# Moving the right-hand tiles of a hybrid encoder layer by 384 bytes, and small edits at its first transfers, at a pass border and at its last gates

## The chip, the cores and the metric

The kernel runs on one core of one Trainium2 chip. The metric is device time in microseconds (us) of one execution. Five engines work side by side and meet only at semaphores: PE (matrix products into PSUM), DVE (vector), ACT (scalar functions and copies), POOL and SP. SP, ACT and POOL also issue DMA transfers, each to its own queue. A product has a stationary operand, loaded into the array ahead of it (the view calls that PEld), and a moving operand that is streamed past it.

## The reference, cut to what matters

```python
h    = rms_norm(x, norm_w)                              # x: 512 tokens x 2048, float32
proj = einsum('bsd,de->bse', h, w_in)                   # w_in: 2048 x 4608
q, k, v, g_attn, xr, g_lru = split(proj)
attn = softmax(rope(norm(q)) rope(norm(k))^T / sqrt(128)) v      # 8 heads, 2 kv heads, 128 wide
lru  = scan_forward(conv(xr)) + scan_backward(conv(xr))          # gated linear recurrences
mixed = concat([rms_norm(attn, attn_norm_w) * silu(g_attn),
                rms_norm(lru,  lru_norm_w)  * silu(g_lru)])      # 512 x 2048
out  = x + einsum('bse,ed->bsd', mixed, w_out)          # w_out: 2048 x 2048
```

Everything is float32. silu(g) is g times sigmoid(g).

## The kernel before, in words

**Three products for one.** An operand in float32 is split into a rounded high part (a copy into `float32r`, mostly on ACT) and the rest (a subtraction on DVE). Each product of 128x128 by 128x512 is then three matmuls: high by high, high by low, low by high. Names with `h` are high parts, with `l` low parts: `wh`/`wl` of weights, `oh`/`ol` of operands of the output product, `mh`/`ml` of the mixed activations, `x2` (shown as `x`) of the input.

**Stages.** The kernel turns x and projects the recurrence input (`proj_feat`), then runs the other projections (`proj_feat`, `proj_tok`) with the recurrence, the rotary embedding and the attention woven into them as work of ACT and DVE, and last the output product (`outputs`). The weights of a chunk come in 512 KB transfers into three `wr` tiles. PE's order is written out by hand for the whole program (`manual_schedule`); SP's at the start, and ACT's, DVE's and SP's in the output stage; elsewhere a scheduler with priorities orders ACT and DVE.

**The first transfers.** `xload` and `wraw` load the first 256 columns of x and the first 256 rows of weights in two halves each: x on SP's queue, weights on ACT's, and the norm weights `nw_st` on ACT's between the two weight halves. PE first runs 13 matmuls on `ones` (`busy(WARM)`) that compute nothing needed, turns `nw_st` into columns (`columns`), turns the first x block (`xturn`), runs 6 more on `ones`, and then begins `proj_feat` (L292).

**The output stage.** It is a seven-product scheme on 2x2 blocks. `seven` and `combine` make seven combinations of each of eight pairs of activations (`build`, the left operands `mh`, `ml`: pairs 0 to 3 lie in pool `fin`, 4 in a ring of pool `hq`, 5 to 7 in pool `out`). Two column groups g of the output are made in two passes each: `P1, Q6, Q5, Q7` and then `P2, Q3, Q4`. `uses` gives the order of the uses: pair i, product k; a use is six matmuls (two strips of 128 tokens, three matmuls each), except that pairs 6 and 7 are kept to the end of each product. `operand` makes the moving operand of use n in the tile n mod 7: tiles 0 to 2 are in `fin`, 3 to 6 in `out`. `prepare` runs six uses ahead. When a product is finished, `done` adds its bank into the output tiles `xt` on DVE. The gates of the last four heads and the left operands 5, 6 and 7 are made by DVE and ACT inside the first pass (`last_gates`), one step at each new pair of the first product.

**Addresses.** Pools are allocated from the left (`cp`, `wr`, `xw`, later `out`) and from the right end (`end`, `hq`, `lru`, `qkv`, `att`, `wx`, `fin`) of each partition's memory. In the built program the tiles of `wr`, `xw` and `out` start at multiples of 512 bytes. Below `end` (24 floats) nearly all tiles of the right-hand pools have remainder 384 after division by 512 (`k2` of pool `att`: 192). So two operands of one matmul can differ in this remainder: a weight from `wx` (right) with `x2` of `xw` (left), or `mh` of `fin` with `oh` of `out`.

Of the kernel before, what the change touches and what calls it, by code (L numbers as in the profile page):

```python
# [11 lines left out]
F32 = mybir.dt.float32  # L12
# [25 lines left out]
AHEAD = 600  # L38


WARM, WARM2 = 13, 6


STEPS = 2
# [12 lines left out]
def hybrid_kernel(  # L57
# [27 lines left out]
    def opened(name, side):  # L85
        pools[name] = tc.alloc_tile_pool(name=name, bufs=1, side=side, reuse_waits="tile")
        order[side].append(name)
        return pools[name]
# [8 lines left out]
    cp = opened("cp", "left")  # L97
    opened("wr", "left")
    opened("xw", "left")
    opened("end", "right").tile([P, 24], F32, tag="end", name="end")  # L100
    hring = opened("hq", "right").ring(8 * 2048, name="hring")
    aring = pools["hq"].ring(8 * 2048, name="aring")
    opened("lru", "right")
# [81 lines left out]
        return vec[:, r : r + 1]  # L185


    def wraw(w, r0, c0, nk=1, queue=nc.sync):

        raw = pools["wr"].tile([P, 2, SEQ], F32, tag="wr", bufs=3, name=nm("wr"))  # L190
        src = w[r0 : r0 + 2 * P, c0 : c0 + SEQ].rearrange("(k p) e -> p k e", p=P)
        for k in range(nk):
            ks = slice(k * 2 // nk, (k + 1) * 2 // nk)
            queue.dma_start(raw[:, ks, :], src[:, ks, :])
            yield raw

    turn_of = [0]

    def wsplit(raw, k):

        turn_of[0] += k
        pool = pools["wx" if "wx" in pools and turn_of[0] % 2 else "xw"]
        hi = pool.tile([P, SEQ], F32R, tag="wh", bufs=4, name=nm("wh"))
        lo = pool.tile([P, SEQ], F32R, tag="wl", bufs=4, name=nm("wl"))
        nc.scalar.copy(hi, raw[:, k, :])  # L205
        nc.vector.tensor_sub(lo, raw[:, k, :], f(hi))  # L206
        return hi, lo

# [6 lines left out]
    xh, xl = [None] * KT, [None] * KT  # L215
    ssq = const([P, NT, KT // 2], "ssq")

    def xload(c, nk=1):

        xc = b4(shape=(P, NT, 2 * P))  # L220
        for k in range(nk):
            ks = slice(k * 2 * P // nk, (k + 1) * 2 * P // nk)
            cs = slice(c * 2 * P + ks.start, c * 2 * P + ks.stop)
            nc.sync.dma_start(xc[:, :, ks], xf[:, cs].rearrange("(t p) d -> p t d", p=P))
            yield xc

    def xturn(xc, kk):
# [339 lines left out]
    def weights(q, g, t):  # L567

        qh, ql = q
        tt = slice(t * P, (t + 1) * P)  # L570
        sc = mm()
        mm3(sc, qh[:, tt], ql[:, tt], kth[g], ktl[g], True, True)
        mx = pools["att"].tile([P, 1], F32, tag="mx", bufs=6, name=nm("mx"))
        nc.vector.tensor_reduce(mx, sc, axis=AX.X, op=ALU.max, negate=True)  # L574
        p = k2()
        sm = pools["att"].tile([P, 1], F32, tag="sm", bufs=6, name=nm("sm"))
        nc.scalar.activation(p, sc, AF.Exp, bias=mx, accum_out=sm)
        nc.vector.reciprocal(sm, sm)
        nc.gpsimd.tensor_scalar(p, p, sm, 0.0, op0=ALU.mult, op1=ALU.add)
        return p  # L580
# [112 lines left out]
    def seven(src, op, hi, lo):  # L693

        src = halves(src)
        res = combine(src, op)
        for to, part in ((slice(0, 3), src[:, 1:4]), (slice(3, 7), res)):
            nc.scalar.copy(hi[:, to], part)
            nc.vector.tensor_sub(lo[:, to], part, f(hi[:, to]))

    def kept(pool, n=7):
        return [pool.tile([P, n, H], F32R, tag=t, bufs=1, name=t) for t in (nm("mh"), nm("ml"))]
# [91 lines left out]

    kept_c = {}
    PASS = (((0, "P1"), (5, "Q6"), (4, "Q5"), (3, "Q7")), ((2, "P2"), (6, "Q3"), (1, "Q4")))
    TAIL = 2

    def uses():

# [39 lines left out]

    def outputs(work):

        bank, tmp, at = {}, {}, [0]

        def take(key):
            bank[key] = pj() if at[0] % 8 >= 4 else mm()
            at[0] += 1
            return bank[key]

        def tm(tag, s):  # L850
            tmp[tag, s] = fin_ev()
            return tmp[tag, s]

        def fin_ev():
            return pools["fin"].tile([P, SEQ], F32, tag="ev", bufs=4, name=nm("ev"))

        def done(g, name, s):

            xt = xts[g]
            b00, b01 = xt[s][:, :SEQ], xt[s][:, SEQ:]  # L860
            b10, b11 = xt[2 + s][:, :SEQ], xt[2 + s][:, SEQ:]
            v = nc.vector
            if name == "P1":
                nc.scalar.copy(tm("a", s), bank[name, s])
                v.tensor_add(b11, b11, tmp["a", s])
            elif name == "Q6":
                v.tensor_sub(tm("b", s), bank[name, s], tmp["a", s])
                v.tensor_sub(b01, b01, tmp["b", s])
            elif name == "Q5":
                v.tensor_add(tm("c", s), bank[name, s], tmp["b", s])  # L870
                v.tensor_add(b00, b00, tmp["c", s])
            elif name == "Q7":
                v.tensor_add(b00, bank[name, s], b00)
                store(g, s, 0)
                v.tensor_sub(b01, b01, bank[name, s])
                v.tensor_add(b10, b10, tmp["c", s])
            elif name == "P2":
                v.tensor_add(b11, bank[name, s], b11)
                store(g, 2 + s, 1)
            elif name == "Q3":  # L880
                v.tensor_add(b10, bank[name, s], b10)
                store(g, 2 + s, 0, queue=nc.sync if g else None)
            elif g == 0 or s == 0:
                v.tensor_add(b01, bank[name, s], b01)
                store(g, s, 1, queue=nc.sync if g else None)
            else:
                for h in range(2):
                    hs = slice(h * H, (h + 1) * H)
                    v.tensor_add(b01[:, hs], bank[name, s][:, hs], b01[:, hs])
                    store(g, s, 1, hs, nc.sync)  # L890

        def mult(use, s):

            g, second, k, i = use
            a, name = PASS[second][k]
            ah, al = mixed[i][1]
            bh, bl = ready[use]
            ts_ = slice(s * P, (s + 1) * P)
            if i == 0:
                take((name, s))  # L900
            for j, (lh, rh) in enumerate(((ah, bh), (ah, bl), (al, bh))):
                nc.tensor.matmul(  # L902
                    bank[name, s], lh[:, a, ts_], rh, start=i == 0 and j == 0,
                    stop=i == 7 and j == 2,
                )
            if i == 7:
                done(g, name, s)

        for n, use in enumerate(order_):
            g, second, k, i = use  # L910
            prepare(n + NW - 1)
            if (second, k, i) == (0, 0, 3):
                xts.setdefault(g, None)
                xts[g] = xts[g] or residual_tiles()
                residual(g)
            if g == 0 and not second and k == 0:
                next(work, None)
            if i < 8 - TAIL:
                for s in range(2):
                    mult(use, s)  # L920
            elif i == 7:
                for s in range(2):
                    for m in range(8 - TAIL, 8):
                        mult((g, second, k, m), s)
# [19 lines left out]
    )  # L944
    given = {}
    with tc.high_priority():
        xs, ws = xload(0, 2), wraw(w_in, 0, C_XR, 2, nc.scalar)
        xc, raw = next(xs), next(ws)
        nc.scalar.dma_start(nw_st, norm_w.rearrange("(k p) -> k p", p=P))
        next(xs), next(ws)  # L950
        table = const([P, 1], "table")
        nc.scalar.activation(table, ones[:, :1], AF.Exp)
        columns(nw, nw_st)
        first = [wsplit(raw, 0)]
        xturn(xc, 0)
        busy(WARM2)
    chunks = [xchunk(c) for c in range(1, KT // 2)]
# [99 lines left out]

    def build(i, pair, where):
        mixed[i][1] = hi, lo = where(7)
        seven(pair, ALU.subtract, hi, lo)  # L1060

    for q in range(4):
        for _ in range(2):
            next(fill, None)
        build(q, hp[q], lambda n: kept(pools["fin"]))
    drain(fill)


    def later():
        for pair in ap_[:2]:  # L1070
            normed(pair)
        yield 6
        todo = gate(late, ap_[:2], R_AN, fin_s)
        for _ in range(3):
            yield next(todo)
        build(4, ap_[0], lambda n: [hring.tile([P, n, H], F32R, name=nm(t)) for t in ("mh", "ml")])
        yield from todo
        for pair in ap_[2:]:
            normed(pair)
# [13 lines left out]
        prepare(NW - 1)  # L1093

    def last_gates():
        yield
        build(5, ap_[1], lambda n: last_mixed[0])
        yield
        todo = gate(gs, ap_[2:], R_AN + 4, fin_s)
        for _ in range(3):  # L1100
            next(todo)
        yield
        build(6, ap_[2], lambda n: last_mixed[1])
        drain(todo)
        yield
        build(7, ap_[3], lambda n: last_mixed[2])
        yield

    with tc.manual_schedule(
        engines={mybir.EngineType.Activation, mybir.EngineType.DVE, mybir.EngineType.SP}  # L1110
# [45 lines left out]
```

## Time and profile before

| | us |
|---|---|
| three runs | 658.4, 656.95, 658.29 |
| median | 658.29 |
| the profiled execution | 657.07 |
| its span from the first to the last instruction | 655.3 |

The profile is of one execution. Times inside it count from the start of its span. "Busy" of PE holds the modelled ends of matmuls; the distance between the starts of two matmuls says more, and the chain of waits shows it: a piece of it lasts from its own start to the next one's.

### The profile page before, as it was taken

Reading aid. Unit: us, or ns where it says so; the run is one execution under the profiler, and the core shown is the slowest. Engines: PE = TensorE matmul, PEld = TensorE weight load, DVE = VectorE, ACT = ScalarE, POOL = GpSimd, SP = SyncE. Lnnn points to the kernel's source line nnn. Section 1 sums busy time; section 2 is a strip of 40 time slices with the busy share of each in tenths; the row PEclk is TensorE's granted clock in tenths of the full one; section 3 lists DMA queues with packets and bytes.
Section 4 is the critical chain, followed back from the end, with each engine's and each line's share of the span. In section 5 each row is a group of like instructions: output and inputs, shape, how many; then the busy total and the mean of one; then the engine's idle time right before and its main releaser. Section 6 shows DMA issues by size and latency. Waiting matters only on the chain.

```text
span 655.3 us, 8600 instructions
## 1 busy us (share of the span) xinstructions
PE 647.8 (99%) x2960; PEld 532.1 (81%) x2960; DVE 485.8 (74%) x832; ACT 344.4 (53%) x639; POOL 96.5 (15%) x127
## 2 busy tenths in 40 slices
PE   8999999999999999999999999999999999999997
PEld 6888888888888888888888888888888878888875
DVE  5778679977687925855955568439948997698994
ACT  3543799489856515454735456335434564344441
POOL 0000000000022312132543435411000000100000
PEclk9999999999999999999999999999999999999999
DMA  9933253322334331446776678663355667585322
GB/s 292 312 107 113 65 139 95 98 65 65 97 114 129 95 98 33 122 141 147 170 177 149 196 150 193 151 144 111 96 191 197 256 208 248 179 297 177 131 78 96
DMA packets 53067, 96.96 MB, mean 148 GB/s; under 512 B 4316, under 2 KB 14688, under 8 KB 52896
## 3 DMA queue, kind: packets, MB, share of 16 engines
q1 hardware_dynamic: 45648, 75.17, 36.2%
q0 software_dynamic: 7056, 20.72, 13.6%
q10 hardware_dynamic: 320, 0.53, 0.3%
q8 instruction: 23, 0.38, 0.2%
q14 instruction: 20, 0.16, 0.1%
HBM read 92.21 MB, written 20.98 MB: 173 GB/s over the span
## 4 chain that ended last, share of the span: by engine, by line
PE 96%; DVE 1%; DMA 1%; issue 1%; ACT 0%; ACTq 0%; DVEq 0%
PE pj L146 20%; PE pj L148 20%; PE pj L147 20%; PE mm L902 12%; PE pj L902 9%; PE mm L146 3%; PE mm L148 3%; PE mm L147 3%; PE mm L586 2%; PE mm L231 1%; PE pj L292 1%; PE mm L534 1%; DMA nw_st<-in_norm_w_dram 1%; DVE ol L717 0%; DMA rw<-in_w_out_dram 0%
## 5 line engine op out<-in xcount | busy, mean ns | idle before, releaser
L146 PE MATMUL pj<-x,wh 128*128 128x512 f32 x376 | 150.5, 400 | 0.0
L148 PE MATMUL pj<-x,wl 128*128 128x512 f32 x376 | 146.8, 390 | 0.0
L147 PE MATMUL pj<-x,wh 128*128 128x512 f32 x376 | 146.6, 390 | 0.0
L205 ACT CAST wh<-wr 128x512 fp32r<-128x512 f32 x144 | 86.1, 618 | 70.4 <-PE pj L148 26.2
L206 DVE TENSOR_TENSOR wl<-wr,wh 128x512 fp32r<-128x512 f32 x144 | 98.7, 706 | 29.7 <-ACT wh L205 29.7
L148 PEld LDWEIGHTS pj<-x,wl 128*128 128x128 f32 x376 | 70.6, 188 | 15.3
L147 PEld LDWEIGHTS pj<-x,wh 128*128 128x128 f32 x376 | 70.8, 188 | 13.5
L146 PEld LDWEIGHTS pj<-x,wh 128*128 128x128 f32 x376 | 70.7, 188 | 13.5
L146 PE MATMUL pj<-wh,x 128*128 128x512 f32 x192 | 75.3, 392 | 0.0
L148 PE MATMUL pj<-wh,x 128*128 128x512 f32 x192 | 75.2, 392 | 0.0
L147 PE MATMUL pj<-wl,x 128*128 128x512 f32 x192 | 75.1, 391 | 0.0
L716 ACT CAST oh<-rw 128x512 fp32r<-128x512 f32 x94 | 54.8, 619 | 32.6 <-PE mm L902 17.7
L717 DVE TENSOR_TENSOR ol<-rw,oh 128x512 fp32r<-128x512 f32 x94 | 60.6, 686 | 9.7 <-ACT oh L716 6.7
L902 PE MATMUL mm<-ol,mh 128*128 128x512 f32 x128 | 50.3, 393 | 0.5 <-DVE ol L717 0.5
L902 PE MATMUL mm<-oh,mh 128*128 128x512 f32 x128 | 50.2, 392 | 0.0
L902 PE MATMUL mm<-oh,ml 128*128 128x512 f32 x128 | 50.2, 392 | 0.0
L588 ACT CAST pt<-mm 128x512 fp32r<-128x512 f32 x32 | 18.7, 586 | 52.7 <-PE mm L586 52.7
L147 PEld LDWEIGHTS pj<-wl,x 128*128 128x128 f32 x192 | 36.1, 188 | 7.9
L146 PEld LDWEIGHTS pj<-wh,x 128*128 128x128 f32 x192 | 36.0, 188 | 7.9
L148 PEld LDWEIGHTS pj<-wh,x 128*128 128x128 f32 x192 | 36.0, 188 | 7.9
L574 DVE TENSOR_REDUCE mx<-mm 128x1 f32<-128x512 f32 x32 | 22.1, 690 | 23.9 <-PE mm L148 23.4
L902 PE MATMUL pj<-ol,mh 128*128 128x512 f32 x96 | 37.9, 394 | 0.0
(207 smaller groups left out, 1110.2 us busy)
## 6 DMA issues: line engine op xcount, KB each, us to landing
wr<-in_w_in_dram SPq DMA_DIRECT2D x71, 512.0 KB, 3.7
rw<-in_w_out_dram SPq DMA_DIRECT2D x63, 256.0 KB, 3.7
ts<-in_w_out_dram POOLq DMA_DIRECT2D x24, 512.0 KB, 6.5
rw<-ts SPq DMA_DIRECT2D x31, 256.0 KB, 4.9
ts<-ts POOLq DMA_DIRECT2D x8, 512.0 KB, 6.1
xt<-in_x_dram SPq DMA_DIRECT2D x8, 512.0 KB, 8.9
b<-in_x_dram SPq DMA_DIRECT2D x7, 512.0 KB, 8.0
out_dram<-xt POOLq DMA_DIRECT2D x12, 256.0 KB, 3.4
```

The costliest lines, as they stand in the source:

```text
L146: nc.tensor.matmul(acc, lh, rh, start=start, stop=False)
L147: nc.tensor.matmul(acc, lh, rl, start=False, stop=False)
L148: nc.tensor.matmul(acc, ll, rh, start=False, stop=stop)
L205: nc.scalar.copy(hi, raw[:, k, :])
L206: nc.vector.tensor_sub(lo, raw[:, k, :], f(hi))
L231: nc.tensor.transpose(pt[:, t * P : (t + 1) * P], xc[:, t, ks], ident)
L574: nc.vector.tensor_reduce(mx, sc, axis=AX.X, op=ALU.max, negate=True)
L586: nc.tensor.transpose(pt[:, s * P : (s + 1) * P], p[:, s * P : (s + 1) * P], ident)
L588: nc.scalar.copy(pth[:, :, tt], p3)
L716: nc.scalar.copy(hi, src)
L717: nc.vector.tensor_sub(lo, src, f(hi))
L902: nc.tensor.matmul(bank[name, s], lh[:, a, ts_], rh, start=i == 0 and j == 0, stop=i == 7 and j == 2,)
```

## The change

It makes these edits:

- `end` grows from 24 to 120 floats, and `mx` and `sm` get 16 buffers instead of 6. In the built program every 512-wide matmul's operands then start at a multiple of 512 bytes.
- The first transfers: the first half of x and then the first half of the weights on SP's queue; `nw_st`, the second half of x and the second half of the weights on ACT's.
- Matmuls on `ones`: 9, 1 and 4 instead of 13 and 6; the 1 stands between `columns` and the first turn of x.
- The first `wh` is copied by DVE instead of ACT.
- In `done` for Q7 the addition of `c` into `b10` is held back and made at the second and third use of the next pass.
- `seven` stops after its combination and after each of its two parts; `last_gates` runs in 13 pieces over the first 22 uses.
- The last four gates: silu on ACT and one DVE operation, instead of sigmoid and two.

```diff
-WARM, WARM2 = 13, 6
+WARM, WARM1, WARM2 = 9, 1, 4
...
-    opened("end", "right").tile([P, 24], F32, tag="end", name="end")
+    opened("end", "right").tile([P, 120], F32, tag="end", name="end")
...
-        for k in range(nk):
+        nk = len(queues)
+        for k, queue in enumerate(queues):
             ks = slice(k * 2 // nk, (k + 1) * 2 // nk)
             queue.dma_start(raw[:, ks, :], src[:, ks, :])
...
-        mx = pools["att"].tile([P, 1], F32, tag="mx", bufs=6, name=nm("mx"))
+        mx = pools["att"].tile([P, 1], F32, tag="mx", bufs=16, name=nm("mx"))
...
         res = combine(src, op)
+        yield
         for to, part in ((slice(0, 3), src[:, 1:4]), (slice(3, 7), res)):
             nc.scalar.copy(hi[:, to], part)
             nc.vector.tensor_sub(lo[:, to], part, f(hi[:, to]))
+            yield
...
-    TAIL = 2
+    TAIL, PIECES, LAST_USE = 2, 13, 22
...
-                v.tensor_add(b10, b10, tmp["c", s])
+                held.append((b10, tmp["c", s]))
...
-            if g == 0 and not second and k == 0:
+            if second and k and held:
+                b10, c = held.pop(0)
+                nc.vector.tensor_add(b10, b10, c)
+            if n * PIECES // LAST_USE != (n - 1) * PIECES // LAST_USE:
                 next(work, None)
...
-        xs, ws = xload(0, 2), wraw(w_in, 0, C_XR, 2, nc.scalar)
+        queues = nc.sync, nc.scalar
+        xs, ws = xload(0, queues), wraw(w_in, 0, C_XR, queues)
+        nc.scalar.dma_start(nw_st, norm_w.rearrange("(k p) -> k p", p=P))
         xc, raw = next(xs), next(ws)
-        nc.scalar.dma_start(nw_st, norm_w.rearrange("(k p) -> k p", p=P))
         next(xs), next(ws)
...
-        first = [wsplit(raw, 0)]
+        busy(WARM1)
+        first = [wsplit(raw, 0, nc.vector.tensor_copy)]
...
     def last_gates():
...
+        yield from build(5, ap_[1], lambda n: last_mixed[0])
+        for i in (6, 7):
+            for e in range(2):
+                k = 2 * (i - 6) + e
+                sg, dst = fin_s(), ap_[i - 4][:, e, :]
+                nc.scalar.activation(sg, gs[k], AF.Silu)
+                nc.vector.scalar_tensor_tensor(
+                    dst, dst, v1(R_AN + 4 + k), sg, op0=ALU.mult, op1=ALU.mult
+                )
+                yield
+            yield from build(i, ap_[i - 4], lambda n: last_mixed[i - 5])
```

The order of ACT at the start, before the change (`wr` are weights as loaded, `nw_st` the norm weights, `table` a dummy that loads ACT's function table):

```order
L194 DMA wr_142<-in_w_in_dram 128x512
L949 DMA nw_st<-in_norm_w_dram 16x128
L194 DMA wr_142<-in_w_in_dram 128x512
L952 ACT_TABLE_LOAD
L952 ACTIVATE table<-ones 128x1
L205 CAST wh_152<-wr_142 128x512
L233 ACTIVATE x_24_161<-mm_156,nw 128x512
```

The same place after the change:

```order
L956 DMA nw_st<-in_norm_w_dram 16x128
L226 DMA b_18_137<-in_x_dram 128x4x128
L195 DMA wr_139<-in_w_in_dram 128x512
L960 ACT_TABLE_LOAD
L960 ACTIVATE table<-ones 128x1
L235 ACTIVATE x_24_158<-mm_153,nw 128x512
L206 CAST wh_174<-wr_139 128x512
```

The norm weights have moved ahead of everything on ACT's queue, the first weights have left it for SP's queue, half of x has come to it, and the first cast of weights has left ACT for DVE.

The order of DVE at the border between the two passes of the second column group, before the change (`xt` are the output tiles, `pj` the finished product Q7, `ol` a low part that PE waits for, `tc` a sum of weight blocks):

```order
L717 TENSOR_TENSOR ol_5828<-rw_5820,oh_5827 128x512
L873 TENSOR_TENSOR xt_5581<-pj_5465,xt_5581 128x512
L875 TENSOR_TENSOR xt_5581<-xt_5581,pj_5465 128x512
L876 TENSOR_TENSOR xt_5583<-xt_5583,ev_5806 128x512
L873 TENSOR_TENSOR xt_5582<-pj_5469,xt_5582 128x512
L875 TENSOR_TENSOR xt_5582<-xt_5582,pj_5469 128x512
L876 TENSOR_TENSOR xt_5584<-xt_5584,ev_5815 128x512
L717 TENSOR_TENSOR ol_5852<-tc_5416,oh_5851 128x512
L717 TENSOR_TENSOR ol_5868<-rw_5863,oh_5867 128x512
L791 TENSOR_TENSOR tc_5474<-tc_5474,rw_5863 128x512
L717 TENSOR_TENSOR ol_5881<-rw_5865,oh_5880 128x512
```

The same place after the change:

```order
L721 TENSOR_TENSOR ol_5819<-rw_5811,oh_5818 128x512
L877 TENSOR_TENSOR xt_5572<-pj_5456,xt_5572 128x512
L879 TENSOR_TENSOR xt_5572<-xt_5572,pj_5456 128x512
L877 TENSOR_TENSOR xt_5573<-pj_5460,xt_5573 128x512
L879 TENSOR_TENSOR xt_5573<-xt_5573,pj_5460 128x512
L721 TENSOR_TENSOR ol_5841<-tc_5407,oh_5840 128x512
L721 TENSOR_TENSOR ol_5857<-rw_5852,oh_5856 128x512
L922 TENSOR_TENSOR xt_5574<-xt_5574,ev_5797 128x512
L795 TENSOR_TENSOR tc_5465<-tc_5465,rw_5852 128x512
L721 TENSOR_TENSOR ol_5871<-rw_5854,oh_5870 128x512
L922 TENSOR_TENSOR xt_5575<-xt_5575,ev_5806 128x512
```

The two additions of `ev` (L876) stood ahead of the first `ol` of the new pass; they now stand behind the second and the third.

PE's order differs only in the matmuls on `ones`, and POOL's not at all.

More of the change, by code (lines that the diff above doesn't have):

```diff
@@ L185, in v1, with wraw @@
         return vec[:, r : r + 1]
-    def wraw(w, r0, c0, nk=1, queue=nc.sync):
+    def wraw(w, r0, c0, queues=(nc.sync,)):
         raw = pools["wr"].tile([P, 2, SEQ], F32, tag="wr", bufs=3, name=nm("wr"))
         src = w[r0 : r0 + 2 * P, c0 : c0 + SEQ].rearrange("(k p) e -> p k e", p=P)
-        for k in range(nk):
+        nk = len(queues)
+        for k, queue in enumerate(queues):
             ks = slice(k * 2 // nk, (k + 1) * 2 // nk)
@@ L197, in hybrid_kernel, with wsplit @@
     turn_of = [0]
-    def wsplit(raw, k):
+    def wsplit(raw, k, rounded=nc.scalar.copy):
         turn_of[0] += k
@@ L204, in wsplit @@
         lo = pool.tile([P, SEQ], F32R, tag="wl", bufs=4, name=nm("wl"))
-        nc.scalar.copy(hi, raw[:, k, :])
+        rounded(hi, raw[:, k, :])
         nc.vector.tensor_sub(lo, raw[:, k, :], f(hi))
@@ L216, in hybrid_kernel, with xload @@
     ssq = const([P, NT, KT // 2], "ssq")
-    def xload(c, nk=1):
+    def xload(c, queues=(nc.sync,)):
         xc = b4(shape=(P, NT, 2 * P))
-        for k in range(nk):
+        nk = len(queues)
+        for k, queue in enumerate(queues):
             ks = slice(k * 2 * P // nk, (k + 1) * 2 * P // nk)
             cs = slice(c * 2 * P + ks.start, c * 2 * P + ks.stop)
-            nc.sync.dma_start(xc[:, :, ks], xf[:, cs].rearrange("(t p) d -> p t d", p=P))
+            queue.dma_start(xc[:, :, ks], xf[:, cs].rearrange("(t p) d -> p t d", p=P))
             yield xc
@@ L572, in weights @@
         mm3(sc, qh[:, tt], ql[:, tt], kth[g], ktl[g], True, True)
-        mx = pools["att"].tile([P, 1], F32, tag="mx", bufs=6, name=nm("mx"))
+        mx = pools["att"].tile([P, 1], F32, tag="mx", bufs=16, name=nm("mx"))
         nc.vector.tensor_reduce(mx, sc, axis=AX.X, op=ALU.max, negate=True)
         p = k2()
-        sm = pools["att"].tile([P, 1], F32, tag="sm", bufs=6, name=nm("sm"))
+        sm = pools["att"].tile([P, 1], F32, tag="sm", bufs=16, name=nm("sm"))
         nc.scalar.activation(p, sc, AF.Exp, bias=mx, accum_out=sm)
@@ L841, in outputs @@
     def outputs(work):
-        bank, tmp, at = {}, {}, [0]
+        bank, tmp, at, held = {}, {}, [0], []
         def take(key):
@@ L1059, in build @@
         mixed[i][1] = hi, lo = where(7)
-        seven(pair, ALU.subtract, hi, lo)
+        return seven(pair, ALU.subtract, hi, lo)
     for q in range(4):
@@ L1064, in hybrid_kernel @@
             next(fill, None)
-        build(q, hp[q], lambda n: kept(pools["fin"]))
+        drain(build(q, hp[q], lambda n: kept(pools["fin"])))
     drain(fill)
@@ L1075, in later @@
             yield next(todo)
-        build(4, ap_[0], lambda n: [hring.tile([P, n, H], F32R, name=nm(t)) for t in ("mh", "ml")])
+        drain(
+            build(4, ap_[0], lambda n: [hring.tile([P, n, H], F32R, name=nm(t)) for t in ("mh", "ml")])
+        )
         yield from todo
@@ L1095, in last_gates @@
     def last_gates():
[L1096 to L1107, printed above, removed]
+        yield from build(5, ap_[1], lambda n: last_mixed[0])
[6 more added lines that the diff above has]
+                    dst, dst, v1(R_AN + 4 + k), sg, op0=ALU.mult, op1=ALU.mult
+                )
+                yield
+            yield from build(i, ap_[i - 4], lambda n: last_mixed[i - 5])
     with tc.manual_schedule(
```

## The prediction

> **What bounds the kernel now.** I read the page's busy time and its chain first: where must a gain come from?
>
> ```profile
> PE 647.8 (99%) x2960; PEld 532.1 (81%) x2960; DVE 485.8 (74%) x832; ACT 344.4 (53%) x639; POOL 96.5 (15%) x127
> PE 96%; DVE 1%; DMA 1%; issue 1%; ACT 0%; ACTq 0%; DVEq 0%
> ```
>
> The first row is busy time of each engine, the second the shares of the chain that ended last. Almost all of the span is PE doing matmuls one behind the other. An edit can only shorten the pace of the matmuls, the few gaps between them, the start, or the end. Next, the chain in the output stage, in order of time: start, length, engine and bank, count. Two uses are 12 matmuls.
>
> ```profile
> 495.19 2.72 PE mm L902 x12
> 497.92 2.75 PE pj L902 x12
> 500.67 2.80 PE mm L902 x12
> 503.47 2.77 PE pj L902 x12
> 506.24 2.72 PE mm L902 x12
> 508.96 2.79 PE pj L902 x12
> 511.75 2.80 PE mm L902 x12
> 514.55 2.73 PE pj L902 x12
> ...
> 645.64 5.47 PE mm L902 x24
> 651.11 0.02 issue
> ```
>
> PE waits for nothing here, yet the same 12 matmuls take 2.72 or 2.80 us, and the pattern is that of the addresses. In these uses the stationary `mh` is always a right-hand tile (remainder 384). The moving `oh` and `ol` of use n are right-hand where n mod 7 is 0, 1 or 2, else left-hand (remainder 0). Row by row, uses with equal remainders: 2 of 2 (n = 0, 1), 1 of 2, 0 of 2, 1 of 2, 2 of 2, 0, 0, 2 of 2. The times follow: 2.72, 2.75, 2.80, 2.77, 2.72, 2.79, 2.80, 2.73. Banks don't (both sorts stand at `mm` and at `pj`). So a matmul costs 2.72/12 = 226.7 ns where both operands start at the same remainder, and 2.80/12 = 233.3 ns where not: 6.6 ns apart.
>
> **The change part by part.** *Addresses.* Afterwards both operands of every 512-wide matmul start at a multiple of 512, so I take 226.7 ns for all. What that is worth, stage by stage, with these rows (windows: length, PE busy and count, the other engines; groups: count, busy, mean ns):
>
> ```profile
> 190.00:260.00 70.00, 70.00 (x317) 57.01 (x316) 45.28 (x85) 36.20 (x107) 16.47 (x24) 1.00 0.32 94
> L148 PE MATMUL pj<-wh,x 128*128 128x512 f32 x95 | 37.5, 394 | 0.0
> L902 PE MATMUL mm<-oh,mh 128*128 128x512 f32 x128 | 50.2, 392 | 0.0
> L902 PE MATMUL pj<-ol,mh 128*128 128x512 f32 x96 | 37.9, 394 | 0.0
> L146 PE MATMUL mm<-kt,b 128*128 128x512 f32 x32 | 12.6, 395 | 0.0
> ```
>
> Output stage: 3 x 128 + 3 x 96 = 672 matmuls from 495.19 to 651.11, 155.9 us. At 226.7 ns they take 152.3. Of the 3.6 us between, 0.8 are the stall below, so 2.8 are pace. From 190 to 260 us weights lie in turn in the right-hand `wx` and the left-hand `xw`; some 283 matmuls (three lines of about 95), so between half and all of them at 6.6 ns: 0.9 to 1.9 us. I take 1.2, nearer to half, since half the weights are in `wx`. Attention: 96 score matmuls with `kt` right-hand and the left operand `b` at remainder 0, 96 x 6.6 ns = 0.6; I take 0.5. Other stages have few such pairs. Sum **4.5 us**; the bounds are 0 (the remainder only goes along with something else) and 5.3. A loss is excluded by the 2.72 rows, in which the remainders are equal already.
>
> A rule of the Trainium skill speaks against this term. SBUF — State Buffer, "Operand start alignment", asks only for a start at a multiple of the element's size, and "Who interferes with whom" gives PE two independent read ports, one for the moving operand and one for the weights, and says that PE never waits on anyone. By it this term would be 0; the trace's 2.72 against 2.80 us does not agree.
>
> *Two additions behind the pass border.* The only stall of PE in the middle of the program is here:
>
> ```profile
> 620.45 0.68 DVE L873 TENSOR_TENSOR xt<-pj,xt 128x512 f32<-128x512 f32 x1
> 621.05 0.68 DVE L875 TENSOR_TENSOR xt<-xt,pj 128x512 f32<-128x512 f32 x1
> 621.64 0.69 DVE L876 TENSOR_TENSOR xt<-xt,ev 128x512 f32<-128x512 f32 x1
> 622.25 0.68 DVE L873 TENSOR_TENSOR xt<-pj,xt 128x512 f32<-128x512 f32 x1
> 622.85 0.68 DVE L875 TENSOR_TENSOR xt<-xt,pj 128x512 f32<-128x512 f32 x1
> 623.44 0.69 DVE L876 TENSOR_TENSOR xt<-xt,ev 128x512 f32<-128x512 f32 x1
> 624.04 0.69 DVE L717 TENSOR_TENSOR ol<-tc,oh 128x512 fp32r<-128x512 f32 x1
> 623.86 0.39 PE L902 MATMUL mm<-oh,mh 128*128 128x512 f32 x1
> 624.78 0.50 PE L902 MATMUL mm<-ol,mh 128*128 128x512 f32 x1 [0.54 <-DVE ol L717]
> ```
>
> Two matmuls start 0.92 us apart instead of 0.23: a loss of 0.69, and the one behind restarts slowly, some 0.1 more. Without the two L876 rows, which each hold DVE for 0.60 until the next start, `ol` ends at about 624.73 - 1.20 = 623.53, ahead of the 624.09 at which PE wants it. Behind it the additions come back: next `ol` to 624.1, addition to 624.7, `tc` to 625.3, third `ol` to 625.9. PE wants that third one for the use that begins at 623.86 + 2 x 1.39 = 626.6. Nothing is late next. Gain **0.7 us**, bounds 0.3 (a new small wait) and 0.8.
>
> *The start.* Timeline rows (start, length) and DMA issues (KB, us from issue to landing):
>
> ```profile
> 1.13 2.96 PE L935 MATMUL mm<-ones 128*128 128x256 bf16 x13 [1.13 <-POOL ones L154]
> 1.18 0.45 ACTq L949 DMA_DIRECT2D nw_st<-in_norm_w_dram  x1
> 5.55 0.20 PE L180 MATMUL mm<-ident,nw_st 16*128 16x16 f32 x1 [1.46 <-DMA nw_st<-in_norm_w_dram]
> 6.17 0.82 PE L935 MATMUL mm<-ones 128*128 128x256 bf16 x6
> 6.38 0.69 ACT L233 ACTIVATE x<-mm,nw 128x512 fp32r<-128x512 f32 x1 [1.30 <-PE mm L231]
> 7.12 1.20 PE L292 MATMUL pj<-x,wh 128*128 128x512 f32 x4
> wr<-in_w_in_dram ACTq DMA_DIRECT2D x1, 256.0 KB, 3.7
> b<-in_x_dram SPq DMA_DIRECT2D x2, 256.0 KB, 4.8
> ```
>
> The norm weights, issued at 1.18 behind 256 KB, hold PE until 5.55; x had landed by then. Issued first on ACT's queue they land long before x. The first half of x stays first on SP's queue. It lands between 4.4 (3.7 us after issue, like the first weights) and 5.5; I take 4.7. Then 0.6 of turning and 0.7 of ACT put `x` at 6.0. The weights now stand second on SP's queue, where x's second half stood, which landed 4.8 us after 1.23, at 6.1. DVE's copy adds at most 0.69 (like the subtraction rows above): `wh` between 5.7 and 6.8. The first needed matmul then starts between 6.0 and 6.8 instead of 7.12; I take 6.5, a gain of **0.6 us**, bounds -0.3 (the weights land at 6.7) and 1.1. From there PE is without gaps, so an earlier start moves everything.
>
> *Last left operands in pieces, silu.* Rows of DVE and ACT in the first pass:
>
> ```profile
> 518.14 0.69 DVE L645 TENSOR_TENSOR av<-av,ev 128x512 f32<-128x512 f32 x1
> 523.88 1.22 DVE L699 TENSOR_TENSOR ml<-t,mh 128x1024 fp32r<-128x1024 f32 x1 [0.25 <-ACT mh L698]
> 525.02 5.50 DVE L717 TENSOR_TENSOR ol<-rw,oh 128x512 fp32r<-128x512 f32 x9
> 2.13 1.28 ACT L952 ACT_TABLE_LOAD   x1 [2.13 <-issue]
> ```
>
> Four multiplications like the first row go (2.8 us of DVE), one load of a function table comes (1.28 us of ACT). PE waits for neither: in the chain above it is continuous. The pieces put operands `ol` of later uses ahead of the last left operand. By the built order DVE has five more of them before it (5 x 5.50/9 = 3.1 us), against 2.8 us of multiplications and a combination made earlier, so its last `ml`, now done at 525.1, comes at about 525 to 526. PE needs it at 495.19 + 24 x 1.36 + 0.7 = 528.5 at the new pace. Counted at **0**, with 2.5 us to spare; if that cover went, each us later would cost one.
>
> The sum is 4.5 + 0.7 + 0.6 = 5.8 us. From the profiled execution (657.07) this gives 651.3; it was 1.2 faster than the median of the three runs (658.29), from which it gives 652.5. I forecast **651.9**.
>
> **Rivals.**
>
> *The remainder is not the cause.* Then only 1.3 us is left: 657.0, no change that can be told. For it: nothing in the rows says how an address would slow PE. Against it: eight pieces in a row follow the addresses.
>
> *The clock comes late.* The first thirteen matmuls on `ones` take 2.96/13 = 0.23 us each, the six later ones 0.82/6 = 0.14: PE's clock rose in between. Nine give PE 9 x 0.23 = 2.1 us of early work instead of 3.0. If the clock is then still low at 6.5, a matmul of 512 columns costs twice what 256 columns cost at first, about 0.45 us instead of 0.23. For 1.3 to 4 us of such time half is lost, 0.7 to 2 us: 652.6 to 653.9. For it: the 1.2 us between runs may be just this. Against it: the one extra matmul and the earlier turns keep PE busy in the gap.
>
> The Trainium skill (TensorE: Matmul & The Clock Gate, Part 1) says that the array starts at half clock and is released after about 3.4 us of sustained work, in windows that don't start with the kernel. The trace's rise agrees; one window more at half clock would put the loss at up to 1.7 us, an estimate from that page.
>
> *The first weights land last.* Four transfers of 256 KB share the engines. If the weights come at 6.7, the first matmul is at 7.4 and the start loses 0.3: 652.8.
>
> *The left operands come late (slower).* The 13 pieces hand over between DVE and ACT, each behind an `oh` that waits for PE to free its tile. If eight such steps each cost one use of 1.36 us, the last `ml` is 10.9 late, 2.5 of them hidden: PE stalls 8.4 us, 658.3 - 5.8 + 8.4 = 660.9. It decides from a delay of 10 us. Against it: six uses are prepared ahead, and DVE has less to do.
>
> **How the numbers follow.** Forecast 0.62; remainder no cause 0.09; clock 0.14; weights last 0.11; left operands 0.04. The range, 650.2 to 654.8: below, 657.07 less 5.3, 0.8 and part of the 1.1 at the start; above, the median's 652.5 with the late clock's 2 and a little. A measurement here tells 0.3% (2 us) from no change: faster 0.87, same 0.09, slower 0.04.
>
> **What would show it.** In the chain after, all pieces of 12 matmuls in the output stage at 2.72, and the stage (to the last matmul) at 152.4 us instead of 155.9; 190 to 260 about 1.2 shorter; no stall of 0.9 us near the last pass border; L294 (the first needed matmul, L292 before) at 6.5. Pieces that still differ by 0.08 would prove the first term wrong; matmuls 0.45 us apart behind the start would show the late clock; waits of PE for `mh` or `ml` the last rival.

## The result

The changed kernel takes 651.18 us (median of 4 runs, 651.15 to 651.27). The kernel before, run beside it, takes 658.35 (656.95 to 658.79). The ratio is 0.9892, with a 95% interval from 0.9877 to 0.9908: 7.2 us faster. The forecast was 651.9 with a range from 650.2 to 654.8. The busy time and the shares of the chain in the profile after:

```profile
PE 644.0 (99%) x2955; PEld 532.6 (82%) x2955; DVE 482.9 (74%) x829; ACT 345.8 (53%) x639; POOL 95.4 (15%) x127
PE 99%; DVE 0%; DVEq 0%; issue 0%; POOL 0%; POOLq 0%
```

The chain is now PE's almost alone: DVE's part is under half a per cent, and that of DMA is gone. The chain of waits in the output stage (start, length, engine and bank, count):

```profile
492.86 2.72 PE mm L906 x12
495.58 2.72 PE pj L906 x12
498.30 2.72 PE mm L906 x12
501.02 2.72 PE pj L906 x12
...
617.98 2.72 PE mm L906 x12
...
645.19 0.02 issue
```

Every piece of 12 matmuls takes 2.72 us, where they took 2.72 to 2.80; the row at 617.98 holds the pass border, where PE had stalled. The stage lasts from 492.86 to 645.19, 152.3 us instead of 155.9. Of the 5.92 us by which its end comes earlier in this profile (651.11 against 645.19), 3.59 are gained in this stage and 2.33 ahead of it. Where those lie is read from matmuls that are the same in both programs. First before, then after (a turn of x near the start, a turn of the queries just ahead of the attention, and a product with ones for the attention's sums near its end):

```profile
37.82 0.88 PE mm L231 x8
...
276.57 0.44 PE mm L534 x4
...
441.08 0.79 PE mm L655 x8
```

```profile
36.90 0.87 PE mm L233 x8
...
274.20 0.44 PE mm L536 x4
...
438.74 0.79 PE mm L657 x8
```

At 37 us the changed kernel is 0.92 ahead, at 276 it is 2.37 ahead, at 441 still 2.34. So the start gave about 0.9, the way from there to the attention about 1.4, and the attention nothing. Of the 1.4, the stretch from 190 to 260 us, with weights in two pools, gave 1.3: PE starts 323 matmuls in these 70 us, where the same row of the kernel before has 317.

```profile
190.00:260.00 70.00, 70.00 (x323) 58.10 (x322) 46.43 (x86) 37.23 (x114) 18.05 (x25) 1.00 0.32 95
```

### The profile page after: what moved, and what is told of

It reads as the page before. It is cut to its first block, busy times and chain, and to the rows that moved or that the text cites. A ratio compares the mean times of both kernels' runs of the same rounds, so it can differ in the third digit from the quotient of the medians.

```text
span 649.4 us, 8581 instructions
## 1 busy us (share of the span) xinstructions
PE 644.0 (99%) x2955; PEld 532.6 (82%) x2955; DVE 482.9 (74%) x829; ACT 345.8 (53%) x639; POOL 95.4 (15%) x127
## 3 DMA queue, kind: packets, MB, share of 16 engines
q1 hardware_dynamic: 45264, 75.17, 36.8%
## 4 chain that ended last, share of the span: by engine, by line
PE 99%; DVE 0%; DVEq 0%; issue 0%; POOL 0%; POOLq 0%
PE pj L146 20%; PE pj L147 20%; PE pj L148 20%; PE mm L906 13%; PE pj L906 10%; PE mm L148 3%; PE mm L147 3%; PE mm L146 3%; PE mm L588 2%; PE mm L233 1%; PE pj L294 1%; PE mm L536 1%; PE mm L942 1%; PE mm L657 0%; DVE xt L893 0%; DVEq L1163 0%
## 5 line engine op out<-in xcount | busy, mean ns | idle before, releaser
L720 ACT CAST oh<-rw 128x512 fp32r<-128x512 f32 x94 | 56.2, 620 | 36.7 <-PE mm L906 17.1
L906 PE MATMUL pj<-oh,ml 128*128 128x512 f32 x96 | 37.4, 389 | 0.0
```

The lines of the kernel that those rows point to most:

```text
L720: nc.scalar.copy(hi, src)
L906: nc.tensor.matmul(bank[name, s], lh[:, a, ts_], rh, start=i == 0 and j == 0, stop=i == 7 and j == 2,)
```

## Experiments on the addresses

**The address edits alone**, on the kernel before:

```diff
-    opened("end", "right").tile([P, 24], F32, tag="end", name="end")
+    opened("end", "right").tile([P, 120], F32, tag="end", name="end")
...
-        mx = ... bufs=6      sm = ... bufs=6
+        mx = ... bufs=16     sm = ... bufs=16
```

> The kernel before with the address edits alone (end at 120 floats, mx and sm with 16 buffers). Theory A (a matmul costs about 6 ns more when the offsets of its two operands differ modulo 512): the output stage, from its first matmul to its last, takes 152.3 us plus the stall of 0.8 at the pass border, 153.1 instead of 155.9; the stretch from 190 us to 262 gets 1.3 shorter; the whole is about 4.3 us faster than before, the start being as before. Theory B (the offset only went along with the other edits): the stage stays at 155.9 and the time does not change.

Measured: 655.03 us against 658.46, ratio 0.9945 [0.9927, 0.9963]. It is 3.4 us faster, not 4.3. The pace came as theory A says, but PE now waited for DVE where it had hardly waited before:

```profile
524.82 0.39 PE L902 MATMUL pj<-oh,mh 128*128 128x512 f32 x1
525.63 0.50 PE L902 MATMUL pj<-ol,mh 128*128 128x512 f32 x1 [0.43 <-DVE ol L717]
...
622.10 0.39 PE L902 MATMUL mm<-oh,mh 128*128 128x512 f32 x1
623.29 0.50 PE L902 MATMUL mm<-ol,mh 128*128 128x512 f32 x1 [0.80 <-DVE ol L717]
```

The starts of the two pairs are 0.81 and 1.19 us apart instead of 0.23. The first place is the one of the last left operands, at which the kernel before lost 0.2 (its row at 525.61 below); the second is the pass border, at which it lost 0.8. With the restarts behind them the two places cost 0.7 and 1.1 here. The faster matmuls come there earlier and DVE does not. Theory B fell.

**All edits but the addresses**, on the changed kernel:

```diff
-    opened("end", "right").tile([P, 120], F32, tag="end", name="end")
+    opened("end", "right").tile([P, 24], F32, tag="end", name="end")
...
-        mx = ... bufs=16     sm = ... bufs=16
+        mx = ... bufs=6      sm = ... bufs=6
```

> The changed kernel with the address edits undone. Theory A: the output stage takes 155.1 us (155.9 less the stall of 0.8), the time is about 4.3 us above the changed kernel's 651.2, so 655.5. Theory B: the stage stays at 152.3 and the time at 651.2.

Measured: 655.31 us, ratio to the kernel before 0.9957 [0.9939, 0.9974]. Beside the next two kernels, whose operands agree in other ways and which ran on the same chip (651.30 and 651.14), the addresses are worth 4.1 us. The chain has the old pattern again, to the hundredth:

```profile
494.54 2.72 PE mm L906 x12
497.27 2.75 PE pj L906 x12
500.02 2.80 PE mm L906 x12
502.82 2.77 PE pj L906 x12
...
649.44 0.02 issue
```

The stage takes 154.9 us, where theory A had 155.1. The 0.2 between them is the wait at the last left operands, which theory A left out. The same piece in the kernel before and in this one:

```profile
525.61 2.97 PE pj L902 x12
524.96 2.79 PE pj L906 x12
```

So of the 3.59 us that the stage gained, 2.6 are pace, 0.8 the pass border and 0.2 this wait.

**All at 384.** Left and right at the same offset, which is no multiple of 512:

```diff
-    opened("end", "right").tile([P, 120], F32, tag="end", name="end")
+    opened("end", "right").tile([P, 24], F32, tag="end", name="end")
...
+    const([P, 96], "shift")
     nw_st = const([KT, P], "nw_st")
```

> The changed kernel with all tiles of 512-wide matmuls, left and right, at offset 384 modulo 512. Theory A1 (only the difference of the two operands counts): as the changed kernel, output stage 152.3 us, time 651.2. Theory A2 (an operand that is not at a multiple of 512 costs): all 672 matmuls of the stage cost 233 ns, 156.8 us, and the whole program up to 2688 x 6.6 ns = 17 us more, 660 to 668.

Measured: 651.30 us, ratio 0.9898 [0.9879, 0.9917]; the output stage, read as above, takes 152.3 us. Theory A1 holds: what counts is not the multiple of 512 but that the operands agree.

**Right-hand tiles at 256**, the left ones at 0:

```diff
-    opened("end", "right").tile([P, 120], F32, tag="end", name="end")
+    opened("end", "right").tile([P, 56], F32, tag="end", name="end")
```

> The changed kernel with the right-hand tiles at offset 256 modulo 512, the left-hand ones at 0. If the unit is 512 bytes: slow as with 384, output stage 155.1 us, time 655.5. If the unit is 256 bytes or less: as the changed kernel, 152.3 and 651.2.

Measured: 651.14 us, ratio 0.9893 [0.9872, 0.9913], as fast as the changed kernel, all pieces at 2.72. The unit is not 512: an offset of 256 between the operands costs nothing.

**Right-hand tiles at 448**, by the same line with 8 floats:

> The changed kernel with the right-hand tiles at offset 448 modulo 512, 64 bytes off the left-hand ones. If the unit is 64 bytes or less: as the changed kernel, output stage 152.3 us, time 651.2. If it is 128 or 256 bytes: slow pairs as with 384, output stage about 154 to 155, time 655.

Measured: 655.61 us, ratio 0.996 [0.9947, 0.9973]. 64 bytes apart costs as much in all as 128 bytes apart, so agreement modulo 64 bytes is not enough. The pattern differs, though:

```profile
495.00 2.73 PE mm L906 x12
497.73 2.75 PE pj L906 x12
500.48 2.75 PE mm L906 x12
503.23 2.76 PE pj L906 x12
505.99 2.74 PE mm L906 x12
...
525.28 2.80 PE pj L906 x12
```

Pieces in which the operands of each matmul agree (first and fifth) cost 2.73 and 2.74 here, and the third, in which they all differ, 2.75, between the two prices of 384. There the stationary operand is the right-hand one. In the last row it is the other way round, the moving operand right-hand and the stationary one (pair 5) left-hand, and 12 matmuls cost 2.80. A distance of 64 bytes so has two prices, by the side that is ahead, which theory A does not say.

## Experiments on the other edits

**The start as before**, in the changed kernel:

```diff
-WARM, WARM1, WARM2 = 9, 1, 4
+WARM, WARM1, WARM2 = 13, 0, 6
...
-        xs, ws = xload(0, queues), wraw(w_in, 0, C_XR, queues)
-        nc.scalar.dma_start(nw_st, norm_w.rearrange("(k p) -> k p", p=P))
+        xs, ws = xload(0, (nc.sync,) * 2), wraw(w_in, 0, C_XR, (nc.scalar,) * 2)
         xc, raw = next(xs), next(ws)
+        nc.scalar.dma_start(nw_st, norm_w.rearrange("(k p) -> k p", p=P))
...
-        first = [wsplit(raw, 0, nc.vector.tensor_copy)]
+        first = [wsplit(raw, 0)]
```

> The changed kernel with the start of before: transfers, 13 and 6 matmuls on ones, first cast on ACT. Theory C (the start is worth what the trace after shows, 0.8 us, when the clock rises early, and about 1.3 us more when it rises late, because 13 matmuls on ones and then a gap leave more needed matmuls behind): runs in two groups as those of the kernel before, at about 652.0 and 653.4. Rival (the order of the transfers is hidden): 651.2.

Measured: 653.36 us (653.05 to 654.42), ratio 0.9926 [0.9913, 0.9938]. The start is worth 2.1 us against the next kernel, which ran on the same chip (651.23) and differs from the changed one in its matmuls on `ones` alone; and the five runs are not in the two groups that theory C names: all lie around the slower of the two (653.4) or above it. The timeline of PE in the slowest of them (654.42) shows why:

```profile
6.52 1.49 PE L942 MATMUL mm<-ones 128*128 128x256 bf16 x6
7.66 2.06 PE L294 MATMUL pj<-x,wh 128*128 128x512 f32 x4
9.51 1.06 PE L233 MATMUL mm<-ident,b 128*128 128x128 f32 x4
10.22 1.85 PE L294 MATMUL pj<-x,wl 128*128 128x512 f32 x4
```

The same six matmuls on `ones` that took 0.82 us in the profile of before take 1.49 here, and the first four needed ones 2.06 instead of 1.20. Matmuls at half pace still stand at 10 us: PE's clock was low. The trace's own record of the granted clock agrees. It begins at 11.67 us in this execution and at 4.37 in the profile of before. So the profile of before shows an execution in which the clock rose early. The address run's profile, with the same start, has a late rise too, at 9.70.

**13 matmuls on `ones` ahead**, none behind the columns:

```diff
-WARM, WARM1, WARM2 = 9, 1, 4
+WARM, WARM1, WARM2 = 13, 0, 4
```

> The changed kernel with 13 matmuls on ones ahead of the columns instead of 9, none behind them. If the clock rises earlier for more early work (by 4.4 us as in the profile of before): the first needed matmul comes at about 5.9 at full pace, 0.4 us faster than the changed kernel, 650.8. If the clock's rise does not depend on these four: the start comes 0.5 us later for nothing, 651.7.

Measured: 651.23 us, ratio 0.9893 [0.9879, 0.9906], no difference to 651.18. In its profile the clock had risen in time, at 5.24 us (the first four needed matmuls took 1.19 us from 6.12 on). The needed matmuls started 0.7 later than in the changed kernel and lost nothing behind, so neither of the two expectations has it: what was gained by the clock was given up by the later start.

**The additions back ahead of the border**:

```diff
-                held.append((b10, tmp["c", s]))
+                v.tensor_add(b10, b10, tmp["c", s])
```

> The changed kernel with the two additions back in front of the pass border. Theory D (DVE's queue at the border holds PE): PE stalls there again, now 1.0 us since it arrives earlier, 652.2. Rival (with fewer other things on DVE they fit): 651.2.

Measured: 652.23 us, ratio 0.9908 [0.9894, 0.9921], 1.0 above the 651.23 of the run beside it. The stall is back:

```profile
619.52 0.39 PE L906 MATMUL mm<-oh,mh 128*128 128x512 f32 x1
620.70 0.50 PE L906 MATMUL mm<-ol,mh 128*128 128x512 f32 x1 [0.80 <-DVE ol L721]
```

1.18 us lie between two starts: 0.95 too many, and nearly 0.2 more behind it. Theory D holds.

**The last gates as before**: whole steps at the first product's uses, sigmoid and two operations of DVE.

```diff
-            if n * PIECES // LAST_USE != (n - 1) * PIECES // LAST_USE:
+            if g == 0 and not second and k == 0:
                 next(work, None)
...
     def last_gates():
+        yield
+        drain(build(5, ap_[1], lambda n: last_mixed[0]))
...
+        todo = gate(gs, ap_[2:], R_AN + 4, fin_s)
...
+        drain(build(7, ap_[3], lambda n: last_mixed[2]))
```

> The changed kernel with the last gates and left operands in whole steps and by sigmoid, as before. As forecast (counted at 0, hidden): 651.2 and no wait of PE. Theory E (hidden at the old pace only; at the new pace DVE has fallen behind by the 24th use, as in the run with the address edits alone): a wait of about 0.7 us near 523 us, 651.9.

Measured: 651.77 us, ratio 0.9901 [0.9886, 0.9917], 0.5 above the 651.23 of the run beside it. That is small, but the wait of theory E is there; read from the starts in the profile, it costs 0.7 with its restart. On PE and, at the same time, on DVE:

```profile
522.49 0.39 PE L906 MATMUL pj<-oh,mh 128*128 128x512 f32 x1
523.32 0.50 PE L906 MATMUL pj<-ol,mh 128*128 128x512 f32 x1 [0.45 <-DVE ol L721]
```

```profile
521.44 1.23 DVE L702 TENSOR_TENSOR ml<-t,mh 128x1024 fp32r<-128x1024 f32 x1 [0.25 <-ACT mh L701]
522.58 1.89 DVE L721 TENSOR_TENSOR ol<-rw,oh 128x512 fp32r<-128x512 f32 x3
```

What PE waits for is not a left operand, but the `ol` of the next use, which stands behind the long `ml` of 1.23 us on DVE. The pieces put `ol` between.

**The changed kernel again, and with the identity matrix moved.** In the changed kernel the identity of the transposes still lies 128 bytes past a multiple of 256.

> The changed kernel itself, beside the next one on the same chip: 651.2 us, attention (from 280 us to 430) at the same pace as in its first trace.

Measured: 651.53 us (651.21 to 652.52), ratio 0.9901 [0.9885, 0.9917]. The profiled execution is the 652.52; its first needed matmuls are

```profile
5.94 2.05 PE L294 MATMUL pj<-x,wh 128*128 128x512 f32 x4 [0.26 <-DVE wh L206]
...
8.49 1.67 PE L294 MATMUL pj<-x,wl 128*128 128x512 f32 x4
```

with the clock still low at 9 us; its record begins at 9.54, against 7.34 in the first profile. The late clock costs the changed kernel too, when it comes that late.

```diff
+    const([P, 32], "pad0")
     ident = const([P, P], "ident")
...
+    const([P, 32], "pad1")
     nw_st = const([KT, P], "nw_st")
```

> The changed kernel with the identity matrix of the transposes, and all operands of matmuls, at multiples of 256 bytes; in the changed kernel the identity lies 128 bytes past one. Theory F (the attention stage gained nothing because the transposes between its matmuls now differ from everything around them): the attention stage gets 0.4 to 0.6 us shorter, the time 650.6. Rival (transposes are too short for it to matter): 651.2.

Measured: 651.25 us, ratio 0.9897 [0.9881, 0.9913]. The attention stage, between the same two matmuls as above:

```profile
274.47 0.44 PE mm L538 x4
...
438.64 0.79 PE mm L659 x8
```

164.17 us, against 164.54 in the changed kernel (274.20 to 438.74) and 164.51 before. 0.37 us shorter, a little under theory F's figure; its total of 650.6 is not met, and 651.25 does not tell the gain from none. The run with all tiles at 384 says the same without a moved identity: there the tiles agree with it modulo 256, since it lies at 128. Between the same two matmuls it takes 164.19 us:

```profile
274.81 0.44 PE mm L537 x4
...
439.00 0.79 PE mm L658 x8
```

In the execution with the identity moved the clock rose early, at 4.74 us, and the start was then held by something else:

```profile
5.64 1.20 PE L296 MATMUL pj<-x,wh 128*128 128x512 f32 x4 [0.34 <-ACT x L237]
8.05 0.62 ACT L208 CAST wh<-wr 128x512 fp32r<-128x512 f32 x1 [2.47 <-DMA wr<-in_w_in_dram]
8.58 0.68 ACT L237 ACTIVATE x<-mm,nw 128x512 fp32r<-128x512 f32 x1
9.31 1.20 PE L296 MATMUL pj<-x,wh 128*128 128x512 f32 x4 [0.19 <-ACT x L237]
```

ACT waits for the second half of the first weights, the last of the four transfers, until 8.05; the second x stands behind that cast, and PE waits for it.

**Both small edits together** (identity moved, 13 matmuls on `ones` ahead):

> The changed kernel with the identity at a multiple of 256 bytes and 13 matmuls on ones ahead of the columns, none behind them: the two edits that did not lose anything alone. If both small gains add (attention 0.3 us, and fewer needed matmuls at half pace): 650.7 to 650.9. If not: 651.2.

Measured: 650.98 us (650.83 to 651.37), ratio 0.9888 [0.9871, 0.9904]. The median is the lowest of all, but 0.2 below the changed kernel is less than its own runs differ. No gain over it can be claimed.

## Why the prediction was right, and where it was not

**The addresses: 4.5 us forecast, 4.1 measured by undoing them.** The mechanism was the one read from the 2.72 and 2.80 rows. The output stage was forecast at 152.3 us and took 152.3.

The stretch with weights in two pools was forecast at 1.2 and gave 1.3, but partly by luck. The forecast let part of its matmuls, nearer half than all, pay 6.6 ns each. Read from the starts in the trace of before, with the addresses of the built program beside them, all of them pay, but less. There the weights change pool every three matmuls, and the 156 matmuls whose operands agree have a median of 233 ns from start to start, the 130 whose operands differ 232; after the change the median is 227. So a matmul's price is not set by its own two operands alone. In the output stage of before, too, the first agreeing matmuls behind differing ones still take 229 to 234 ns on average, and 227 comes only later.

The attention's 0.5 was wrong: that stage did not move (164.51 and 164.54). Two steps failed. The price: the 96 score matmuls took 230.4 ns on average before and 227.9 after, so they gave 2.5 ns each instead of 6.6, in all 0.24 us. And the forecast counted them alone. It left out the transposes between the matmuls, whose identity stayed 128 bytes off. In the kernel before, the values and the softmax's transposed weights lay at 384 and so agreed with it modulo 256, and the tile to be turned was 64 bytes off; after the change all are 128 off. The transposes themselves did not get slower, but the 304 projection matmuls on high parts of weights, which stand between them, went from 238.3 to 239.8 ns, a loss of 0.46 us. With the identity moved, and with all tiles at 384, they take 238.2. So the loss hangs on where the identity lies against the tiles around it.

The rival that the remainder is no cause fell: its 657.0 is not met, and where PE did not wait, the pieces of the output stage in which all operands agreed modulo 256 took 2.72 to 2.74 us in every layout, and the others up to 2.80. The Trainium skill (SBUF — State Buffer, "Who interferes with whom") gives PE two independent read ports and says that PE never waits on anyone; by it the term would have been 0. The rows of 2.72 and 2.80 us and the 4.1 us of the whole kernel do not agree with it, and the measurement decides. Why PE is slower there is not shown.

**The additions: 0.7 forecast, 0.8 gained at the border.** The stall was removed as reckoned, and nothing took its place. At the new pace the additions would have cost 1.0 by the medians and 1.1 at the border, as the run that puts them back shows.

**The last left operands: counted at 0, and worth 0.5.** The cover was checked at the old pace, with PE against the last `ml`. The piece of 2.97 us at 525.61 in the old profile, where PE lost 0.2 on an `ol`, was the warning, and "PE waits for neither" overlooked it. The new pace used up that cover, and the wait was for the `ol` behind the `ml`, not for the `ml`. That the term was nothing for PE holds for the changed kernel only because the pieces came with the addresses. The rival of late left operands fell: in the changed kernel the last `ml` is done at 522.98, ahead of the 525 to 526 forecast.

```profile
521.75 1.23 DVE L702 TENSOR_TENSOR ml<-t,mh 128x1024 fp32r<-128x1024 f32 x1 [0.26 <-ACT mh L701]
```

**The start: 0.6 forecast, 0.9 in the profile, 2.1 by undoing it.** This is the term that was mis-sized. The first needed matmul began at 5.42 instead of the forecast 6.5, since the first `wh` was there at 5.26 (4.83 and 0.43), not between 5.7 and 6.8. Of the 1.7 us of earlier start 0.9 were lost at once, because the clock was late:

```profile
4.83 0.43 DVE L206 CAST wh<-wr 128x512 fp32r<-128x512 f32 x1 [1.17 <-DMA wr<-in_w_in_dram]
5.42 2.06 PE L294 MATMUL pj<-x,wh 128*128 128x512 f32 x4
```

The four matmuls took 2.06 us instead of 1.20. So the rival of the late clock came true in part, but its price is paid by the kernel before as well, and more often: the profile of before is of an execution in which the clock rose early (657.07, the median of the kernel 658.35). The sum was made from that execution, and 5.9 us is what the two profiles differ by; the other 1.3 of the measured 7.2 is most likely the clock in the runs of the kernel before that have no profile, since both other profiles with the old start show a late rise. And where the clock is early, the other step fails: "from there PE is without gaps" does not hold, since the second half of the weights lands at 8 us and caps the gain. Late clock and late weights so hide each other. In the ten profiles with the new transfers and a rise between 4.60 and 7.73 us, the turn of x of the result section begins between 36.8 and 37.4; with the rise at 9.54 it begins at 38.3. With the old start it begins at 37.8, 39.1 and 40.2 for rises at 4.37, 9.70 and 11.67, so the latest rise costs 2.4 us against the earliest, more than the 0.7 to 2 that the rival allowed. That the late weights hide a rise by 7.7 us is probably why the changed kernel's first four runs agree within 0.12 us where those of the kernel before differ by 1.8.

**The sum.** Between the two profiles the forecast was 5.8 us and 5.9 came. That is close in part by luck: the attention gave 0.5 less than forecast and the pace of the output stage 0.2 less (2.6 for 2.8), and the start, the stretch with two pools, the border and the wait at 525 us gave about 0.1 to 0.3 more each. Undone one at a time the four parts are worth 4.1, 2.1, 1.0 and 0.5, 7.7 in all, and together 7.2. The address edits alone bring 3.4: what they free is held by DVE until the other two edits come.

## What to carry to other kernels

Read the pace of matmuls from starts, not from busy shares: an engine at 99% can still lose 2% of a stage to where its operands lie, and pieces of equal count in the chain show it. Let the two operands of matmuls, transposes included, agree in their start modulo 256 bytes (here that shortened a stage of 672 matmuls by 2.6 us, from 154.9 to 152.3). When the bound engine gets faster, check every cover again at the new pace: two waits on DVE of 0.2 and 0.8 us became 0.7 and 1.1.

## What the runs showed of the hardware that was not expected

The price of disagreeing operands is not one step: 12 matmuls take 2.72 us when both start alike, 2.80 when they differ by 128 bytes modulo 256, about 2.75 or 2.80 when they differ by 64, by the side that is ahead, and 2.72 when they differ by 256. It also reaches matmuls whose own operands agree, when differing ones stand just ahead: in the layout with 64 such pieces cost 2.73 to 2.74, and between 190 and 260 us of the kernel before agreeing matmuls were as slow as the others. Whether a matmul's moving operand meets its own weights or those loaded behind it for the next was not tried.

PE's clock rises at a time that differs from run to run of one program. Of the changed kernel two profiles exist: in one (rise at 7.34 us) the first four needed matmuls, from 5.42 on, and nothing behind them ran slowly; in the other (rise at 9.54) those from 5.94 and the next ones up to 9.5 us. The times of the two executions are 1.4 us apart. The first matmul stands at 1.13 us in all profiles, so the rise came 3.2 us behind it at the earliest (the kernel before) and 10.5 at the latest (the old start in the changed kernel). Four matmuls on `ones` more ahead showed no effect on the time.
